# Mean of ReLU over rows: 127 rows a partition in place of 128, the first 128 rows one to a partition

## Chip, cores, metric

One core of one Trainium2 chip. The metric is the device time of one execution in microseconds; the profile's span is some 1.8 us shorter, as it goes from the first to the last instruction. Every run here is of a fast state, with a granted clock of 1.000.

Some words. DVE is VectorE, ACT is ScalarE, POOL is GpSimd. A partition is one of the 128 rows of on-chip memory; the pitch is the distance in HBM between the starts of two neighbouring partitions. A load runs on 16 DMA engines; it has landed when the last of the 16 is done, and its spread is the time from the first of the 16 landings to the last. The last whole row is the last row that is loaded in one piece; one more follows in column pieces. A fetch is a packet of the page's queue of kind "instruction".

## The reference

```python
batch, seq, dim = 32, 512, 1024
x = np.random.randn(batch, seq, dim).astype(np.float32)

def reference(x):
    relu_x = np.maximum(x, 0)
    return np.mean(relu_x, axis=-1).astype(np.float32)
```

So 16,384 rows of 4 KB are read, 64 MB, and one number a row is written.

## The kernel before

Partition p holds the rows 128p to 128p + 127. Seven full tiles of 16 rows a partition (8 MB) are loaded into three buffers. The last 16 rows come in pieces that get smaller, so that little is left to compute after the last landing. ACT takes the even rows and DVE the odd ones, each with an instruction that sums the row as it clips it; POOL scales the sums.

```python
def act_row(nc, src, acc):
    nc.scalar.activation(out=src, in_=src, func=ACT.Relu, accum_out=acc)

def dve_row(nc, src, acc, init=None):
    nc.vector.tensor_scalar(out=src, in0=src, scalar1=0.0, scalar2=init,
                            op0=ALU.max, op1=ALU.add, accum_out=acc)
# ... (the first load is moved ahead of the entry barrier)
    J = R // P                                             # 128
    xr = xf.rearrange("(p j) d -> p j d", p=P, j=J)        # pitch 512 KB
    outr = out.flatten().rearrange("(p j) -> p j", p=P, j=J)
    NB = 16
    full = J // NB - 1                                     # 7
    row_pieces = [8, 4, 2, 1]
    col_pieces = [512, 256, 256]
# ...
    for t in range(full):
        j0 = t * NB
        xt = in_pool.tile([P, NB, D], F32, name="xt")      # bufs=3
        nc.sync.dma_start(out=xt, in_=xr[:, j0:j0 + NB, :])
        rows(xt, 0, NB, j0)
# ... (loads of the last tile: row pieces, then column pieces of the last row)
    for n in row_pieces[:-1]:
        rows(xt, lo, n, j0)
        lo += n
    finish(j0, j0 + lo)
    act_row(nc, prev[:, :512], part[:, 0:1])               # last whole row: two halves
    dve_row(nc, prev[:, 512:], part[:, 1:2])
# ... (POOL adds and scales; the last row by columns, with partial sums chained on DVE)
    nc.sync.dma_start(out=outr, in_=res)
```

Of the kernel before, what the change touches and what calls it, by code (L numbers as in the profile page):

```python
# [1 line left out]

# [4 lines left out]

F32 = mybir.dt.float32
ALU = mybir.AluOpType
ACT = mybir.ActivationFunctionType  # L10
# [9 lines that stand above are left out]
    nc.vector.tensor_scalar(  # L20
        out=src, in0=src, scalar1=0.0, scalar2=init,
        op0=ALU.max, op1=ALU.add, accum_out=acc,
    )


def issue_ahead_of_entry_barrier(nc):


    entry, body = nc.cur_f.blocks[0].instructions, None
    for block in nc.cur_f.blocks[1:]:  # L30
        for k, ins in enumerate(block.instructions):
            if ins.opcode == "DMACopy":
                body, load = block.instructions, k
                break
        if body is not None:
            break
    first = body[load]
    assert first.engine == mybir.EngineType.SP and not first.sync_info.on_wait
    assert all(i.opcode == "DMACopy" or i.engine != first.engine for i in body[:load])
    del body[load]  # L40
    at = next(k for k, i in enumerate(entry) if i.engine == first.engine and i.opcode == "Drain")
    entry.insert(at, first)


@with_exitstack
def kernel(
    ctx: ExitStack,
    tc: tile.TileContext,
    x: bass.AP,
    out: bass.AP,  # L50
):
    nc = tc.nc
    P = nc.NUM_PARTITIONS
    xf = x.flatten_outer_dims()
    R, D = xf.shape
    assert R % P == 0
    J = R // P
    inv = 1.0 / D
    xr = xf.rearrange("(p j) d -> p j d", p=P, j=J)
    outr = out.flatten().rearrange("(p j) -> p j", p=P, j=J)  # L60
    xlast = xr[:, J - 1, :]

    NB = 16
    full = J // NB - 1

    row_pieces = [8, 4, 2, 1]
    assert sum(row_pieces) == NB - 1
    col_pieces = [512, 256, 256]
    assert sum(col_pieces) == D

    pools = ctx.enter_context(ExitStack())
    in_pool = pools.enter_context(tc.tile_pool(name="in", bufs=3))
    res_pool = pools.enter_context(tc.tile_pool(name="res", bufs=1))
    sums = res_pool.tile([P, J], F32)
    res = res_pool.tile([P, J], F32)
    part = res_pool.tile([P, 10], F32)

    def rows(xt, lo, n, j0):

        for k in range(lo, lo + n):  # L80
            j = j0 + k
            (dve_row if j % 2 else act_row)(nc, xt[:, k, :], sums[:, j:j + 1])

    def finish(lo, hi):
        nc.gpsimd.tensor_scalar(  # L85
            out=res[:, lo:hi], in0=sums[:, lo:hi], scalar1=inv, scalar2=0.0, op0=ALU.mult, op1=ALU.add,
        )

    for t in range(full):
        j0 = t * NB  # L90
        xt = in_pool.tile([P, NB, D], F32, name="xt")
        nc.sync.dma_start(out=xt, in_=xr[:, j0:j0 + NB, :])  # L92
        rows(xt, 0, NB, j0)

    j0 = full * NB
    xt = in_pool.tile([P, NB, D], F32, name="xt")
    prev, last = xt[:, NB - 2, :], xt[:, NB - 1, :]
    lo = 0
    for n in row_pieces:
        nc.sync.dma_start(out=xt[:, lo:lo + n, :], in_=xr[:, j0 + lo:j0 + lo + n, :])  # L100
        lo += n
    c = 0
    for w in col_pieces:
        nc.sync.dma_start(out=last[:, c:c + w], in_=xlast[:, c:c + w])
        c += w

    finish(0, j0)
    lo = 0
    for n in row_pieces[:-1]:
        rows(xt, lo, n, j0)  # L110
        lo += n
    finish(j0, j0 + lo)



    act_row(nc, prev[:, :512], part[:, 0:1])
    dve_row(nc, prev[:, 512:], part[:, 1:2])
    nc.gpsimd.tensor_scalar(  # L118
        out=res[:, J - 2:J - 1], in0=part[:, 0:1], scalar1=part[:, 1:2], scalar2=inv, op0=ALU.add, op1=ALU.mult,
    )  # L120
    act_row(nc, last[:, :256], part[:, 2:3])
    dve_row(nc, last[:, 256:512], part[:, 3:4])
    nc.gpsimd.tensor_scalar(  # L123
        out=part[:, 4:5], in0=part[:, 2:3], scalar1=inv, scalar2=0.0, op0=ALU.mult, op1=ALU.add,
    )
    act_row(nc, last[:, 512:640], part[:, 5:6])
    dve_row(nc, last[:, 640:768], part[:, 6:7], init=part[:, 3:4])
    nc.scalar.activation(  # L128
        out=part[:, 7:8], in_=part[:, 5:6], func=ACT.Identity, scale=inv, bias=part[:, 4:5],
    )  # L130
    dve_row(nc, last[:, 768:], part[:, 8:9], init=part[:, 6:7])
    nc.vector.scalar_tensor_tensor(  # L132
        out=res[:, J - 1:J], in0=part[:, 8:9], scalar=inv, in1=part[:, 7:8], op0=ALU.mult, op1=ALU.add,
    )
    nc.sync.dma_start(out=outr, in_=res)

    pools.close()
    tc.close()
    tc.compile()
    issue_ahead_of_entry_barrier(nc)  # L140


# [1 line left out]
_INS = ['x']  # L144
_OUTS = [((32, 512), 'float32')]


# [23 lines left out]
```

## Time and profile before

| | before |
|---|---|
| time, median of 3 | 164.05 us (163.62 to 164.06) |
| DVE, ACT busy | 46%, 43% |
| the 16 DMA engines busy with the loads | 96.6% |
| last landing of x | 158.62 us |
| last instruction of DVE | 159.43 to 159.59 us |
| the store of the result | issued 159.65, landed 161.19 us |

The kernel is one stream of loads with a short end behind it. The lines that carry this stand in the prediction below; what the landings say to a hundredth of a microsecond comes from the semaphore and packet records of the trace, which the views show only through the instructions that wait for them.

### The profile page before, as it was taken

What the parts mean: (1) busy time and instruction counts of PE and PEld (TensorE: products, weight loads), DVE (VectorE), ACT (ScalarE), POOL (GpSimd) and SP (SyncE); (2) the same over time, 40 slices, a digit from 0 to 9 for tenths busy, and PEclk for the clock granted to TensorE, in tenths of its full rate; (3) what the DMA queues carried; (4) which work ended last, traced back from release to release, by engine and by line L of the source; (5) the groups of instructions that cost most, each with busy time, mean ns of one, the idle gap of its engine ahead of it and who ended that gap; (6) DMA issues with size and microseconds to landing.
All of it is one profiled execution on the core that took longest, in us unless ns stands there. A gap on an engine that the chain in (4) does not pass through costs nothing.

```text
span 162.1 us, 358 instructions
## 1 busy us (share of the span) xinstructions
DVE 74.7 (46%) x135; ACT 69.6 (43%) x134; POOL 1.2 (1%) x8
## 2 busy tenths in 40 slices
DVE  0000049700795009930199102990049800698993
ACT  3000049500793009910199002980049600696882
POOL 0000000000000000000000000000000000000001
DMA  8996996997997998998998999899898897998980
GB/s 275 501 485 291 518 501 291 501 501 323 469 518 340 437 518 356 420 518 356 420 520 374 404 501 404 388 501 404 388 518 388 388 518 332 437 445 384 420 311 17
DMA packets 2162, 67.19 MB, mean 415 GB/s; under 512 B 240, under 2 KB 624, under 8 KB 880
## 3 DMA queue, kind: packets, MB, share of 16 engines
q1 hardware_dynamic: 2160, 67.18, 96.6%
q14 instruction: 2, 0.02, 0.0%
HBM read 67.11 MB, written 0.07 MB: 414 GB/s over the span
## 4 chain that ended last, share of the span: by engine, by line
DMA 84%; DVE 13%; SPq 1%; issue 0%; DVEq 0%
DMA xt<-in_x_dram 84%; DVE xt L20 13%; SPq L100 1%; DVE res L132 0%; DVEq L20 0%; DVEq L132 0%; SPq L92 0%
## 5 line engine op out<-in xcount | busy, mean ns | idle before, releaser
L20 DVE TENSOR_SCALAR_CACHE_REDUCE xt<-xt 128x1024 f32<-128x1024 f32 (+1 forms) x65 | 73.7, 1195 | 84.7 <-DMA xt<-in_x_dram 84.3
L15 ACT ACTIVATE xt<-xt 128x1024 f32<-128x1024 f32 (+1 forms) x66 | 67.0, 1015 | 88.7 <-DMA xt<-in_x_dram 88.6
L15 ACT ACTIVATION_READ_ACCUMULATOR xt<-xt 128x1 f32 x66 | 12.3, 186 | 0.0
L20 DVE DVE_READ_ACCUMULATOR xt<-xt 128x1 f32 x65 | 5.4, 83 | 0.0
L85 POOL TENSOR_SCALAR res<-sums 128x112 f32<-128x112 f32 (+1 forms) x2 | 0.5, 252 | 156.7 <-DVE xt L20 156.7
L15 ACT ACT_TABLE_LOAD x1 | 1.3, 1283 | 0.8 <-PEq L155 0.8
L20 DVE TENSOR_SCALAR_CACHE_REDUCE xt<-xt,part 128x128 f32<-128x128 f32 (+1 forms) x2 | 0.8, 412 | 0.1
L128 ACT ACTIVATE part<-part 128x1 f32<-128x1 f32 x1 | 0.3, 294 | 0.1
L118 POOL TENSOR_SCALAR res<-part 128x1 f32<-128x1 f32 x1 | 0.3, 264 | 0.5 <-ACT xt L15 0.5
L132 DVE SCALAR_TENSOR_TENSOR res<-part 128x1 f32<-128x1 f32 x1 | 0.2, 159 | 0.1
L123 POOL TENSOR_SCALAR part<-part 128x1 f32<-128x1 f32 x1 | 0.2, 191 | 0.1
L20 DVE DVE_READ_ACCUMULATOR xt<-xt,part 128x1 f32 x2 | 0.2, 83 | 0.0
L155 POOL MEMSET const-bfloat16-1.0<- 128x1 bf16 x1 | 0.1, 101 | 0.0
L155 POOL MEMSET const-uint8-127<- 128x1 uint8 x1 | 0.1, 101 | 0.0
L155 POOL MEMSET const-float32-0.0<- 128x1 f32 x1 | 0.1, 98 | 0.2 <-issue 0.2
L155 POOL MEMSET const-float32-1.0<- 128x1 f32 x1 | 0.1, 98 | 0.0
## 6 DMA issues: line engine op xcount, KB each, us to landing
xt<-in_x_dram SPq DMA_DIRECT2D x1, 4096.0 KB, 39.0
xt<-in_x_dram SPq DMA_DIRECT2D x1, 2048.0 KB, 43.5
xt<-in_x_dram SPq DMA_DIRECT2D x1, 1024.0 KB, 45.5
xt<-in_x_dram SPq DMA_DIRECT2D x1, 512.0 KB, 46.4
xt<-in_x_dram SPq DMA_DIRECT2D x1, 256.0 KB, 46.5
xt<-in_x_dram SPq DMA_DIRECT2D x2, 128.0 KB, 42.7
xt<-in_x_dram SPq DMA_DIRECT2D x7, 49.1
out_dram<-res SPq DMA_DIRECT2D x1, 64.0 KB, 1.5
```

The costliest lines, as they stand in the source:

```text
L15: nc.scalar.activation(out=src, in_=src, func=ACT.Relu, accum_out=acc)
L20: nc.vector.tensor_scalar(out=src, in0=src, scalar1=0.0, scalar2=init, op0=ALU.max, op1=ALU.add, accum_out=acc,)
L85: nc.gpsimd.tensor_scalar(out=res[:, lo:hi], in0=sums[:, lo:hi], scalar1=inv, scalar2=0.0, op0=ALU.mult, op1=ALU.add,)
L100: nc.sync.dma_start(out=xt[:, lo:lo + n, :], in_=xr[:, j0 + lo:j0 + lo + n, :])
L118: nc.gpsimd.tensor_scalar(out=res[:, J - 2:J - 1], in0=part[:, 0:1], scalar1=part[:, 1:2], scalar2=inv, op0=ALU.add, op1=ALU.mult,)
L123: nc.gpsimd.tensor_scalar(out=part[:, 4:5], in0=part[:, 2:3], scalar1=inv, scalar2=0.0, op0=ALU.mult, op1=ALU.add,)
L128: nc.scalar.activation(out=part[:, 7:8], in_=part[:, 5:6], func=ACT.Identity, scale=inv, bias=part[:, 4:5],)
L132: nc.vector.scalar_tensor_tensor(out=res[:, J - 1:J], in0=part[:, 8:9], scalar=inv, in1=part[:, 7:8], op0=ALU.mult, op1=ALU.add,)
L155: nc = _bacc.Bacc("TRN2", target_bir_lowering=False, num_devices=1)
```

## The change

The 128 rows at the front of x are now one to a partition and are loaded behind the first full tile; the others are 127 to a partition. The starts of the partitions in HBM then lie 508 KB apart rather than 512 KB. That this is the intent is my reading. The first rows get their mean on DVE, with a transpose to bring 128 results from 128 partitions into four rows, and a store of their own on ACT's queue. The last tile has 15 rows instead of 16, in pieces of 8, 4, 1, 1 and the last row.

```diff
-    xr = xf.rearrange("(p j) d -> p j d", p=P, j=J)
-    outr = out.flatten().rearrange("(p j) -> p j", p=P, j=J)
+    outf = out.flatten()
+    M = J - 1
+    xr = xf[P:, :].rearrange("(p j) d -> p j d", p=P, j=M)
+    outr = outf[P:].rearrange("(p j) -> p j", p=P, j=M)
+    xfirst = xf[:P, :]
+    outfirst = outf[:P].rearrange("(q i) -> q i", i=32)
...
-    row_pieces = [8, 4, 2, 1]
+    row_pieces = [8, 4, 1, 1]
...
         rows(xt, 0, NB, j0)
+        if t == 0:
+            x0 = res_pool.tile([P, D], F32)
+            mean0 = res_pool.tile([P, 32], F32)
+            turned0 = res_pool.tile([P, 32], F32)
+            nc.sync.dma_start(out=x0, in_=xfirst)
+            nc.vector.memset(mean0, 0.0)
+            dve_row(nc, x0, mean0[:, 0:1])
+            nc.vector.tensor_scalar_mul(out=mean0[:, 0:1], in0=mean0[:, 0:1], scalar1=inv)
+            nc.vector.transpose(turned0, mean0)
+            nc.scalar.dma_start(out=outfirst, in_=turned0[0:P:32, :])
...
-    for n in row_pieces[:-1]:
+    for n in row_pieces[:2]:
         rows(xt, lo, n, j0)
         lo += n
     finish(j0, j0 + lo)
-    act_row(nc, prev[:, :512], part[:, 0:1])
-    dve_row(nc, prev[:, 512:], part[:, 1:2])
+    for k in range(2):
+        act_row(nc, xt[:, lo + k, :512], part[:, 2 * k:2 * k + 1])
+        dve_row(nc, xt[:, lo + k, 512:], part[:, 2 * k + 1:2 * k + 2])
...  (POOL adds the halves of both rows; the rest renumbers columns)
```

More of the change, by code (lines that the diff above doesn't have):

```diff
@@ L58 @@
     inv = 1.0 / D
-    xr = xf.rearrange("(p j) d -> p j d", p=P, j=J)
-    outr = out.flatten().rearrange("(p j) -> p j", p=P, j=J)
-    xlast = xr[:, J - 1, :]
+    outf = out.flatten()
[4 more added lines that the diff above has]
+    outfirst = outf[:P].rearrange("(q i) -> q i", i=32)
+    xlast = xr[:, M - 1, :]
     NB = 16
-    full = J // NB - 1
-    row_pieces = [8, 4, 2, 1]
-    assert sum(row_pieces) == NB - 1
+    full = M // NB
+    row_pieces = [8, 4, 1, 1]
+    assert full * NB + sum(row_pieces) + 1 == M
     col_pieces = [512, 256, 256]
@@ L73 @@
     res_pool = pools.enter_context(tc.tile_pool(name="res", bufs=1))
-    sums = res_pool.tile([P, J], F32)
-    res = res_pool.tile([P, J], F32)
-    part = res_pool.tile([P, 10], F32)
+    sums = res_pool.tile([P, M], F32)
+    res = res_pool.tile([P, M], F32)
+    part = res_pool.tile([P, 12], F32)
     def rows(xt, lo, n, j0):
@@ L93 @@
         rows(xt, 0, NB, j0)
+        if t == 0:
[8 more added lines that the diff above has]
+            nc.scalar.dma_start(out=outfirst, in_=turned0[0:P:32, :])
     j0 = full * NB
     xt = in_pool.tile([P, NB, D], F32, name="xt")
-    prev, last = xt[:, NB - 2, :], xt[:, NB - 1, :]
+    last = xt[:, NB - 2, :]
     lo = 0
@@ L112 @@
     finish(j0, j0 + lo)
-    act_row(nc, prev[:, :512], part[:, 0:1])
-    dve_row(nc, prev[:, 512:], part[:, 1:2])
+    for k in range(2):
+        act_row(nc, xt[:, lo + k, :512], part[:, 2 * k:2 * k + 1])
+        dve_row(nc, xt[:, lo + k, 512:], part[:, 2 * k + 1:2 * k + 2])
+        nc.gpsimd.tensor_scalar(
+            out=res[:, j0 + lo + k:j0 + lo + k + 1], in0=part[:, 2 * k:2 * k + 1],
+            scalar1=part[:, 2 * k + 1:2 * k + 2], scalar2=inv, op0=ALU.add, op1=ALU.mult,
+        )
+    act_row(nc, last[:, :256], part[:, 4:5])
+    dve_row(nc, last[:, 256:512], part[:, 5:6])
     nc.gpsimd.tensor_scalar(
-        out=res[:, J - 2:J - 1], in0=part[:, 0:1], scalar1=part[:, 1:2], scalar2=inv, op0=ALU.add, op1=ALU.mult,
+        out=part[:, 6:7], in0=part[:, 4:5], scalar1=inv, scalar2=0.0, op0=ALU.mult, op1=ALU.add,
     )
-    act_row(nc, last[:, :256], part[:, 2:3])
-    dve_row(nc, last[:, 256:512], part[:, 3:4])
-    nc.gpsimd.tensor_scalar(
-        out=part[:, 4:5], in0=part[:, 2:3], scalar1=inv, scalar2=0.0, op0=ALU.mult, op1=ALU.add,
-    )
-    act_row(nc, last[:, 512:640], part[:, 5:6])
-    dve_row(nc, last[:, 640:768], part[:, 6:7], init=part[:, 3:4])
-    nc.scalar.activation(
-        out=part[:, 7:8], in_=part[:, 5:6], func=ACT.Identity, scale=inv, bias=part[:, 4:5],
-    )
-    dve_row(nc, last[:, 768:], part[:, 8:9], init=part[:, 6:7])
+    act_row(nc, last[:, 512:640], part[:, 7:8])
+    dve_row(nc, last[:, 640:768], part[:, 8:9], init=part[:, 5:6])
+    nc.scalar.activation(
+        out=part[:, 9:10], in_=part[:, 7:8], func=ACT.Identity, scale=inv, bias=part[:, 6:7],
+    )
+    dve_row(nc, last[:, 768:], part[:, 10:11], init=part[:, 8:9])
     nc.vector.scalar_tensor_tensor(
-        out=res[:, J - 1:J], in0=part[:, 8:9], scalar=inv, in1=part[:, 7:8], op0=ALU.mult, op1=ALU.add,
+        out=res[:, M - 1:M], in0=part[:, 10:11], scalar=inv, in1=part[:, 9:10], op0=ALU.mult, op1=ALU.add,
     )
```

## The prediction

> **What bounds the kernel now.** I read the page first, for who is busy. The two compute engines are at 46% and 43%, while the queue that loads x takes 96.6% of the time of the 16 DMA engines. The chain of work that ended last says the same.
>
> ```profile
> DVE 74.7 (46%) x135; ACT 69.6 (43%) x134; POOL 1.2 (1%) x8
> q1 hardware_dynamic: 2160, 67.18, 96.6%
> DMA 84%; DVE 13%; SPq 1%; issue 0%; DVEq 0%
> ```
>
> The 13% of DVE in the chain is not compute that bounds: the chain leads through buffer reuse, from the release of a buffer to the load that goes into it, and such a load lies behind one or two others in the queue anyway. So I looked next at the timeline of DVE, at the first instruction on each tile, which starts when the tile has landed (columns: start, length, instruction, in brackets how long DVE sat idle before it and for what).
>
> ```profile
> 41.68 1.22 DVE L20 TENSOR_SCALAR_CACHE_REDUCE xt<-xt 128x1024 f32<-128x1024 f32 x1 [10.12 <-DMA xt<-in_x_dram]
> 61.03 1.22 DVE L20 TENSOR_SCALAR_CACHE_REDUCE xt<-xt 128x1024 f32<-128x1024 f32 x1 [10.15 <-DMA xt<-in_x_dram]
> ...
> 100.36 1.22 DVE L20 TENSOR_SCALAR_CACHE_REDUCE xt<-xt 128x1024 f32<-128x1024 f32 x1 [10.64 <-DMA xt<-in_x_dram]
> 119.71 1.22 DVE L20 TENSOR_SCALAR_CACHE_REDUCE xt<-xt 128x1024 f32<-128x1024 f32 x1 [10.15 <-DMA xt<-in_x_dram]
> 139.06 1.22 DVE L20 TENSOR_SCALAR_CACHE_REDUCE xt<-xt 128x1024 f32<-128x1024 f32 x1 [10.14 <-DMA xt<-in_x_dram]
> ```
>
> A tile of 8,388,608 bytes lands every 19.35 us, that is 433.5 GB/s, and DVE idles 10 us in each. One stream of loads, never interrupted, sets the time to about 158.6 us (last landing). Last I read the end, where the stream is over, in the same timeline.
>
> ```profile
> 153.56 1.22 DVE L20 TENSOR_SCALAR_CACHE_REDUCE xt<-xt 128x1024 f32<-128x1024 f32 x1
> 154.70 0.08 DVE L20 DVE_READ_ACCUMULATOR xt<-xt 128x1 f32 x1
> 154.70 1.21 DVE L20 TENSOR_SCALAR_CACHE_REDUCE xt<-xt 128x1024 f32<-128x1024 f32 x1
> 155.84 0.08 DVE L20 DVE_READ_ACCUMULATOR xt<-xt 128x1 f32 x1
> 156.05 1.22 DVE L20 TENSOR_SCALAR_CACHE_REDUCE xt<-xt 128x1024 f32<-128x1024 f32 x1
> 157.19 0.08 DVE L20 DVE_READ_ACCUMULATOR xt<-xt 128x1 f32 x1
> 157.34 0.69 DVE L20 TENSOR_SCALAR_CACHE_REDUCE xt<-xt 128x512 f32<-128x512 f32 x1
> ...
> 157.97 0.42 DVE L20 TENSOR_SCALAR_CACHE_REDUCE xt<-xt 128x256 f32<-128x256 f32 x1
> ...
> 158.83 0.48 DVE L20 TENSOR_SCALAR_CACHE_REDUCE xt<-xt,part 128x256 f32<-128x256 f32 x1
> 158.87 0.29 ACT L128 ACTIVATE part<-part 128x1 f32<-128x1 f32 x1
> 159.23 0.08 DVE L20 DVE_READ_ACCUMULATOR xt<-xt,part 128x1 f32 x1
> 159.43 0.16 DVE L132 SCALAR_TENSOR_TENSOR res<-part 128x1 f32<-128x1 f32 x1
> 159.65 0.35 SPq L135 DMA_DIRECT2D out_dram<-res  x1
> ```
>
> From 157.34, where the last whole row (cut in two halves) has landed, DVE works practically without a gap to 159.59; the column pieces (landed at 157.95, 158.31 and 158.62 by the semaphore records of the trace) meet a DVE that is still busy. So the end hangs on the landing of that row plus the DVE work after it. Before it DVE catches up by 0.1 to 0.2 us on each piece. That is all the slack there is.
>
> **What the Trainium skill says.** (1) "DMA: Bandwidth & Descriptors", section "Latency and other measured facts", on the row pitch in HBM: copies of 128 partitions of 16 KiB with a pitch of 512 KiB a partition ran at 207 GB/s per direction, against 214 with a padded pitch. 128 rows of 4 KB are a pitch of 512 KiB, and 127 rows make it 508 KiB: this is, I think, the intent of the change, and it promises 3%. (2) The same page, "Where 436 GB/s comes from", puts the limit of the 16 ports at 435.2 GB/s, 27.2 a port. The trace sides with the second. The packet records have 64 KB packets at a median of 2418 ns and 32 KB ones at 1213.5; 32,768 bytes in the difference of 1204.5 ns are 27.2 GB/s. The engines already move bytes at the limit of their ports, at the pitch of 512 KiB, so no penalty of the pitch is to be seen that could be removed. (3) The same page, "Why a DMA increments its semaphore by 16 and not by 1": the number of engines that a transfer uses is the largest one up to 16 that divides the slowest dimension of both sides, and 127 partitions would use one engine. Here 127 is the count of rows inside a partition and 128 partitions stay outermost, so I expect 16 engines; before has 16 landings for every load. (4) The same page, "Specifications": under 512 B a transfer takes a read and a write. The last store has 128 packets of 512 B before and of 508 B after. Nothing in the trace of before tests it.
>
> **The change part by part.**
>
> The stream. Row count is the same: 112 + 8 + 4 + 2 + 1 + 1 before, 112 + 1 (first rows, behind tile 0) + 8 + 4 + 1 + 1 + 1 after. A piece of two rows becomes two single ones. By the packet records, an engine takes 8 packets of 311 ns and a 9 ns semaphore write for the two-row piece, 2497 ns; and 8 × 161 + 9 = 1297 ns for a one-row piece, twice 2594. The stream becomes 0.10 us longer. The store of the first 128 results is 4 packets of 128 B, nothing beside the rest, and it lies in the middle.
>
> The work on the first rows. One DVE row (1215 + 83 ns from the groups), a scale on 128x1 (about 159 ns, as the small DVE instruction on line 132), a memset and a 32-wide transpose (an estimate of under 350 ns each, the time of the 128x128 form): some 2 us, in the 10 us that DVE idles after tile 0. ACT issues one DMA and waits for the transpose until about 34 us; its next tile lands near 43. The reuse of tile 0's buffer waits for the tile's own rows, and two tiles are queued ahead of it. Cost 0.
>
> The end. Call X the landing of the last single row: 157.31 + 0.10 = 157.41. The single row before it lands at X − 1.30 and the four-row piece at X − 2.59 = 154.82 (before: 153.54, with 2.49 us to the next piece and 1.28 more to the last row). DVE starts on its two rows of the four at 154.85, and at 1.14 us each it is free at 157.13. Before, by then, the two-row piece and the last row had one whole row in front of X. Now the half of the first single row comes first, 0.63 us (157.34 to 157.97 in the timeline), so DVE is at the last whole row at 157.76, not at 157.34: 0.42 later, of which 0.10 is the stream. The rest, 2.25 us of a DVE that is never idle, follows unchanged. ACT is shorter, 1.04 us a row, and ends in front of it; the extra POOL instruction (264 ns) is off the path.
>
> The store. 508 B packets in place of 512: I add 0.1 for it as a guess between nothing and 1 us. Before, its packets took 27 ns each, and 1.5 us passed from issue to landing.
>
> Sum: 0.10 + 0.32 + 0.1 = about 0.5 us on 164.05: 164.5.
>
> **The rivals.** First, the pitch is a cost and its removal a gain of 2 to 3%. For it: the page of the skill, and the effort that the change makes to get an odd pitch. Against it: the packets are at the rate of the port, and their times hardly vary (2415 lowest, 2418 median). The mean of the 64 KB packets is 2435, so all that lies above the floor is 56 packets an engine × 17 ns, 0.9 us, most of which is the first packet of each engine (about 3.1 us rather than 2.4, the latency of a start). It could make at best 163.5. Second, the store in packets under 512 B becomes read-modify-write in series: 8 packets an engine, an HBM round trip each, would add 1 to 2 us: 165.5 to 166.5. For it, the page; against it, nothing that I have. Third, the new pitch itself reads worse (each 64 KB run now starts at a multiple of 4 KB only): 1% slower packets would add 1.5 us; nothing in the trace speaks for it, as short packets from 1 KB up have the same rate per byte. Fourth, chance in the fetch of instructions. Two such packets of 8 KB at 84.3 and 86.7 us lie between the loads on two of the engines; after them the spread of the 16 landings of a tile grows from 0.83 to 1.34 us and the pace has its one step of 19.85 us. This is worth 0.4 to 0.5 us, and with other instructions it can fall on another engine: either way.
>
> **Range and chances.** The deterministic part is +0.4; store and fetch spread it by some half a microsecond to either side, the three runs of before by 0.4. Eight in ten for 163.9 to 165.4. Faster by 2% would be under 160.8, which is less than the bytes at 433.5 GB/s (154.8 us) plus start and end as they are (2.6 and 5.5 us or more): 1%. Slower by 2% is over 167.3 and needs the store or the pitch to go badly wrong: 3%. Within 2%: 96%.
>
> **What would show it.** The stream: tiles in the middle still land 19.3 to 19.4 us apart and 64 KB packets keep about 2418 ns; if they shorten, the pitch was a cost and I am wrong on what matters most. The end: the half-row instructions on 128x512 come twice, DVE has no idle time between the four-row piece and the last instruction, and the second half-row starts some 0.35 us after its row's landing. The store: 1.5 us from issue to landing now, up to 1.7 after; 2.5 or more means the read-modify-write rival. The first rows: DVE and ACT still idle over 7 us before the second tile. A load that used fewer than 16 engines would show as a tile that takes many times longer, and would make everything above wrong.

## The result

| | before | after |
|---|---|---|
| time, median | 164.01 us (163.62 to 164.06, 4 runs) | 163.83 us (163.77 to 163.95, 4 runs) |
| ratio, 95% interval | | 0.9996 (0.9978 to 1.0013) |

A ratio is the mean time of one kernel's fast runs over the mean of the other's fast runs in the same rounds, so it is not quite the ratio of the medians. The time is the same. I had expected 0.5 us more, and 163.83 is just under the low end of my range (163.9); by the ratio, 0.9996 of the 164.05 that the prediction started from is 163.98, just inside it. The sign of a half microsecond is too small a thing for the class of the result, but where did it go?

The page of the changed kernel: the loads still take nearly all of the DMA engines' time, and the second queue, for the small store, is there with its 8 packets.

```profile
DVE 75.6 (47%) x140; ACT 68.9 (43%) x134; POOL 1.4 (1%) x9
q1 hardware_dynamic: 2304, 67.17, 96.8%
q10 hardware_dynamic: 8, 0.00, 0.0%
```

The timeline of DVE, first instruction on each of the first five tiles after the change:

```profile
22.10 1.22 DVE L20 TENSOR_SCALAR_CACHE_REDUCE xt<-xt 128x1024 f32<-128x1024 f32 x1 [21.15 <-DMA xt<-in_x_dram]
42.73 1.22 DVE L20 TENSOR_SCALAR_CACHE_REDUCE xt<-xt 128x1024 f32<-128x1024 f32 x1 [9.84 <-DMA xt<-in_x_dram]
62.07 1.22 DVE L20 TENSOR_SCALAR_CACHE_REDUCE xt<-xt 128x1024 f32<-128x1024 f32 x1 [10.14 <-DMA xt<-in_x_dram]
81.52 1.22 DVE L20 TENSOR_SCALAR_CACHE_REDUCE xt<-xt 128x1024 f32<-128x1024 f32 x1 [10.25 <-DMA xt<-in_x_dram]
101.23 1.22 DVE L20 TENSOR_SCALAR_CACHE_REDUCE xt<-xt 128x1024 f32<-128x1024 f32 x1 [10.50 <-DMA xt<-in_x_dram]
```

and the two of before that the prediction did not show, the first tile and the one ahead of the slow step:

```profile
22.36 1.22 DVE L20 TENSOR_SCALAR_CACHE_REDUCE xt<-xt 128x1024 f32<-128x1024 f32 x1 [22.36 <-DMA xt<-in_x_dram]
...
80.51 1.22 DVE L20 TENSOR_SCALAR_CACHE_REDUCE xt<-xt 128x1024 f32<-128x1024 f32 x1 [10.27 <-DMA xt<-in_x_dram]
```

The pace between tiles is unchanged (19.34 us from 42.73 to 62.07), and the second tile is 1.31 us later relative to the first, for the load of the first rows. But the first tile lands 0.26 us earlier (22.10 against 22.36), and the one slow step, from the fourth to the fifth tile, is 19.71 us in place of 19.85. By the semaphore records the last tile takes 1.21 us less from its four-row piece to the last whole row (2.57 against 3.78), so the extra packets cost 0.10 us; without these the stream is 0.44 us ahead of before at the last whole row. The end itself, in the same timeline:

```profile
154.43 1.22 DVE L20 TENSOR_SCALAR_CACHE_REDUCE xt<-xt 128x1024 f32<-128x1024 f32 x1
...
155.57 1.21 DVE L20 TENSOR_SCALAR_CACHE_REDUCE xt<-xt 128x1024 f32<-128x1024 f32 x1
...
156.71 0.68 DVE L20 TENSOR_SCALAR_CACHE_REDUCE xt<-xt 128x512 f32<-128x512 f32 x1
...
157.32 0.68 DVE L20 TENSOR_SCALAR_CACHE_REDUCE xt<-xt 128x512 f32<-128x512 f32 x1
...
159.37 0.16 DVE L151 SCALAR_TENSOR_TENSOR res<-part 128x1 f32<-128x1 f32 x1
```

There is no idle time of DVE from 154.43 on, as predicted. The last whole row had landed at 156.97 (semaphore record), and DVE comes to it at 157.32, 0.35 us later. Before, it landed at 157.31 and DVE was there at 157.34. So DVE starts it at the same moment in both: the new end costs 0.35 us, and a stream that is earlier by 0.34 pays for it. The question for the chip is whether the earlier stream is a gain of the change or luck of one trace.

### The profile page after: what moved, and what is told of

Its sections match the earlier page's. It is cut to its first block, busy times and chain, and to the rows that moved or that the text cites. A ratio compares the mean times of both kernels' runs of the same rounds, so it can differ in the third digit from the quotient of the medians.

```text
span 162.0 us, 369 instructions
## 1 busy us (share of the span) xinstructions
DVE 75.6 (47%) x140; ACT 68.9 (43%) x134; POOL 1.4 (1%) x9
## 4 chain that ended last, share of the span: by engine, by line
DMA 83%; DVE 14%; issue 1%; SPq 0%; DVEq 0%
DMA xt<-in_x_dram 83%; DVE xt L20 14%; SPq L117 0%; SPq L105 0%; DVE res L151 0%; DVEq L20 0%; SPq L97 0%; DVEq L151 0%
## 5 line engine op out<-in xcount | busy, mean ns | idle before, releaser
L20 DVE TENSOR_SCALAR_CACHE_REDUCE xt<-xt 128x1024 f32<-128x1024 f32 (+2 forms) x65 | 72.9, 1187 | 82.8 <-DMA xt<-in_x_dram 82.7
L15 ACT ACTIVATE xt<-xt 128x1024 f32<-128x1024 f32 (+2 forms) x66 | 66.5, 1009 | 89.1 <-DMA xt<-in_x_dram 89.1
L20 DVE TENSOR_SCALAR_CACHE_REDUCE x<-x 128x1024 f32<-128x1024 f32 x1 | 1.2, 1219 | 0.0
```

## The experiments

The theories: **A**, the start and the fetch of instructions differ by chance from run to run, and the change costs what I predicted; **B**, the pitch of 512 KB does cost time, and leaving it pays for the new end; **C**, what slows the tile near 90 us is a fetch of instructions on the DMA engines, and how much it costs depends on which engine it meets. Twelve runs were made, each on one chip and with rounds of the kernel before. All were timed in 5 rounds, and every one has the profile of one execution. The traced execution is not always a typical one: where it was the slowest of its run, the text says so. Some give a wrong result, as is said of each.

### Both kernels once more

No edit.

> The kernel before, unchanged, once more. In its first trace the 16 loads of the first tile had all landed at 22.34 us and the last whole row at 157.31. Theory A (start and instruction fetch differ by chance from run to run): another trace of it lands the first tile somewhere between 22.0 and 22.4, and the last whole row between 156.8 and 157.4, not at the same place. Theory B (the pitch of 512 KB makes its start slow): the first tile at 22.3 to 22.4 again. The time against itself: 1.000.

Measured: ratio to itself 0.9998 (0.9985 to 1.0010). First tile at 22.14 us, last whole row at 157.56, the slow step 20.14 us long. The traced execution was the slowest of its five (164.12 us, the median 163.79).

> The changed kernel, unchanged, once more. In its first trace the first tile had landed at 22.08 and the last whole row at 156.97, with DVE only at it at 157.32. Theory A: the first tile anywhere between 22.0 and 22.4. Theory B: at 22.05 to 22.1 again. Both: DVE takes the last whole row some 0.35 us after the landing if that is early, and the ratio to the kernel before is 0.998 to 1.002.

Measured: ratio 1.0004 (0.9992 to 1.0017). First tile at 22.16, last whole row at 157.06, DVE at it at 157.38, 0.32 us late; the slow step 19.68 us.

The first tile of before moved by 0.2 us between two traces, and both first tiles lie outside what B expected and inside what A did (though 157.56 for the last whole row is later than A allowed); single traces cannot tell A from B on the start. That the last whole row lands earlier after the change, by 0.34 us in the first pair of traces, came again, with 0.50; part of that is the slow execution of before.

### The new order at the old pitch

One row of the last tile is loaded behind the first tile and the last tile is cut as after the change; the pitch stays at 512 KB and the store at 512 B. The result is correct.

```diff
-    row_pieces = [8, 4, 2, 1]
+    row_pieces = [8, 4, 1, 1]
...
         rows(xt, 0, NB, j0)
+        if t == 0:
+            x0 = res_pool.tile([P, D], F32)
+            nc.sync.dma_start(out=x0, in_=xr[:, full * NB, :])
+            dve_row(nc, x0, sums[:, full * NB:full * NB + 1])
-    j0 = full * NB
+    j0 = full * NB + 1
...  (the end as in the changed kernel)
```

> The order of loads and the end of the changed kernel, at the old pitch of 512 KB (one row of the last tile is loaded behind the first tile). Theory B, the pitch pays for what the new end costs: first tile at 22.3 to 22.4, ratio to the kernel before 1.002 to 1.003 (the 0.42 us of the prediction). Theory A: as the changed kernel, 0.998 to 1.002. Both: DVE is at the last whole row 0.3 to 0.4 us after it has landed.

Measured: ratio 1.0018 (1.0005 to 1.0032), 0.30 us slower. First tile at 22.31. DVE was at the last whole row at 157.69, 0.35 us after its landing at 157.34. This is the cost that the prediction worked out (0.42, inside the interval of 0.08 to 0.52), seen alone:

```profile
157.69 0.68 DVE L20 TENSOR_SCALAR_CACHE_REDUCE xt<-xt 128x512 f32<-128x512 f32 x1
```

### The pitch alone

The kernel before with the starts of the partitions 127 rows apart. It reads some rows twice, so the result is wrong: the last row of a partition is the first of the next, so the two reads lie at the two ends of the stream. Its instructions stand in the same order on DVE and on the load queue, and its packets have the same sizes.

```diff
-    xr = xf.rearrange("(p j) d -> p j d", p=P, j=J)
+    xr = bass.AP(xf.tensor, 0, [[(J - 1) * D, P], [D, J], [1, D]])
```

> The kernel before with one number changed: the partitions' starts in x lie 127 rows apart, not 128 (so it reads some rows twice and the result is wrong on purpose; every instruction, size and wait is that of before). Theory B, the pitch of 512 KB makes the start slow: in three traces at 512 KB the sixteenth engine's first packet began at 2.16, 2.38 and 2.47 us and the first tile had landed at 22.34, 22.14 and 22.31; in three at 508 KB at 1.66, 1.40 and 1.40, and 22.07, 22.16 and 22.16. Then here the sixteenth first packet begins before 1.7, the first tile lands by 22.2, and the whole is 0.1 to 0.4 us faster than before (ratio 0.9975 to 0.999). Theory A, chance: like before, ratio 1.000, the sixteenth first packet anywhere.

Measured: ratio 0.9974 (0.9961 to 0.9986), 0.42 us faster. **This settles B against A**: one number of the change is worth about what the prediction missed. The profile shows only part of the place. The sixteenth first packet began at 1.69 us, as expected, but the first tile had landed at 22.27, no better than before. The slow step is short in the timeline of DVE:

```profile
80.47 1.22 DVE L20 TENSOR_SCALAR_CACHE_REDUCE xt<-xt 128x1024 f32<-128x1024 f32 x1 [10.27 <-DMA xt<-in_x_dram]
100.07 1.22 DVE L20 TENSOR_SCALAR_CACHE_REDUCE xt<-xt 128x1024 f32<-128x1024 f32 x1 [10.39 <-DMA xt<-in_x_dram]
```

The same two in the repeated kernel before, at 512 KB:

```profile
80.45 1.22 DVE L20 TENSOR_SCALAR_CACHE_REDUCE xt<-xt 128x1024 f32<-128x1024 f32 x1 [10.29 <-DMA xt<-in_x_dram]
100.59 1.22 DVE L20 TENSOR_SCALAR_CACHE_REDUCE xt<-xt 128x1024 f32<-128x1024 f32 x1 [10.93 <-DMA xt<-in_x_dram]
```

19.60 us against 20.14 in that slow execution, and against 19.85 in the first trace of before. A packet of 64 KB took 2418 ns in the median in both kernels, and 2437 in the mean against 2435 and 2436 in the two traces of before, so the gain is not in the time of the packets. This part of the prediction holds.

### A contiguous stream

The seven full tiles as contiguous blocks of 8 MB, so a pitch of 64 KB; the order of rows is wrong.

```diff
+    xb = xf.rearrange("(t p j) d -> t p j d", p=P, j=16)
...
-        nc.sync.dma_start(out=xt, in_=xr[:, j0:j0 + NB, :])
+        nc.sync.dma_start(out=xt, in_=xb[t])
```

> The kernel before with the seven full tiles read as contiguous blocks of 8 MB, so a pitch of 64 KB (wrong order of rows, wrong on purpose; the last tile as before). If what 508 KB does is only to leave the pitch of 512 KB, this start is like that of 508 KB: sixteenth first packet before 1.7 us, first tile by 22.2, ratio as in the run with the pitch alone. If 512 KB is no worse than any other, no difference from before: 1.000. The tiles in the middle stay 19.35 us apart under every theory, as the ports set that.

Measured: ratio 0.9984 (0.9970 to 0.9997), 0.26 us faster. It had the earliest first tile of all (21.92), but its slow step was 20.01 us. The expectation that the tiles in the middle stay 19.35 us apart failed: the second to the fourth landed 19.43, 19.51 and 19.59 us after the one before. (The traced execution was the slowest of its five, 164.14 us, the median 163.75.) So 508 KB is not a lucky pitch; 512 KB is a little worse than two others (the last tile here was still read at 512). How much each of them is worth, these intervals do not separate.

### Few instructions, at both pitches

One instruction of 8 rows for each engine and full tile in place of 8, so that the programs are short; the sums are wrong. Once in the kernel before, once in the changed one.

```diff
-        rows(xt, 0, NB, j0)
+        act_row(nc, xt[:, :8, :].rearrange("p k d -> p (k d)"), sums[:, j0:j0 + 1])
+        dve_row(nc, xt[:, 8:, :].rearrange("p k d -> p (k d)"), sums[:, j0 + 1:j0 + 2])
```

> The kernel before with one instruction of 8 rows an engine for each full tile in place of 8 (the sums are wrong on purpose), so that the programs are too short for a fetch of instructions amid the loads. Theory C, the fetch delays the engine it falls on and the last engine sets every landing: the fetch packets near 85 us are gone, no tile takes over 19.4 us, the spread of the 16 landings stays under 0.9 us to the end, and the kernel is 0.5 to 0.8 us faster (ratio 0.995 to 0.997). If the step in the pace near 90 us has another cause, it stays.

Measured: ratio 0.9967 (0.9955 to 0.9980), 0.54 us faster. The page of before has two packets of instructions:

```profile
q14 instruction: 2, 0.02, 0.0%
```

This line is gone from the page here, and the step with it (timeline of DVE):

```profile
80.60 8.69 DVE L20 TENSOR_SCALAR_CACHE_REDUCE xt<-xt 128x8192 f32<-128x8192 f32 x1 [10.78 <-DMA xt<-in_x_dram]
99.94 8.69 DVE L20 TENSOR_SCALAR_CACHE_REDUCE xt<-xt 128x8192 f32<-128x8192 f32 x1 [10.65 <-DMA xt<-in_x_dram]
```

19.34 us, like any other. **C holds.** The packet records of before show how. They do not name the engines, but an engine's next packet is recorded as starting 3 ns before the end of its last, so that the 16 can be told apart. Two packets of 8 KB and 309 ns, at 84.3 and 86.7 us, each fall on one engine, and the load packet behind each is longer too, 2708 and 3046 ns in place of 2418: the two engines lose 0.60 and 0.94 us. A delayed engine costs only what it lacks in lead over the slowest. The second one had a lead of 0.50 us, which leaves 0.44; the tile landed 0.51 us late, and the spread went from 0.83 to 1.34 us. The delay was not made up: at the last whole row the spread was still 1.33.

> The changed kernel with the same few long instructions (wrong sums on purpose). Theory C: no fetch, no slow tile, 0.3 us faster than the changed kernel (its step was 0.33 us in all three traces at 508 KB, against 0.50, 0.79 and 0.51 at 512 KB). Between this and the run before with few instructions the fetch is out, so what is left is the prediction's sum: 0.10 for the stream, 0.35 for the late DVE, about 0.1 for the store, less what the start gains: 0.3 to 0.5 slower than the other if the start is the same, about 0.3 if the pitch gains 0.15 at the start.

Measured: ratio 0.9983 (0.9970 to 0.9996), 0.28 us faster than the kernel before, and 0.2 to 0.3 faster than the changed kernel itself (0.9996 and 1.0004, in other rounds). Against the run above it is 0.26 us slower: with the fetch out of both, the change costs, though less than the 0.5 of my sum. The first tile landed at 22.00 here and at 22.39 there.

### The pitch alone, with few instructions

The wrong kernel before with few instructions, and the starts 127 rows apart.

```diff
-    xr = xf.rearrange("(p j) d -> p j d", p=P, j=J)
+    xr = bass.AP(xf.tensor, 0, [[(J - 1) * D, P], [D, J], [1, D]])
...  (and one instruction of 8 rows, as above)
```

> The kernel before with few long instructions and the starts of the partitions 127 rows apart (sums wrong on purpose), so the pitch alone where no fetch of instructions falls into the loads. The kernel before with few instructions was 0.9967 of before. If the gain of the pitch of 0.42 us is part start (0.18 us by the landings of the first tile, 22.30 in the mean of five traces at 512 KB against 22.12 in seven at 508) and part a smaller loss to the fetch (0.28), only the start is left here: 0.9956, first tile near 22.1, and 0.2 us between the two. If the fetch has no part in it, the whole gain stays: 0.994. If the start has none either: 0.9967.

Measured: ratio 0.9952 (0.9937 to 0.9967), 0.25 us less than the 0.9967 of its twin (other rounds and another chip, so only roughly). Some gain seems to stay where no fetch is, less than the 0.42, but the two intervals overlap: neither is shown. Its trace is an outlier against the theory of the start: the first tile at 22.46 us, the sixteenth first packet at 2.06. The profiled execution was also the slowest of its six (163.53; the others 162.96 to 163.18).

### Pieces of 7, 4, 2 and 1

The changed kernel with a whole row between the four-row piece and the last whole row, as before the change. Correct.

```diff
-    row_pieces = [8, 4, 1, 1]
+    row_pieces = [7, 4, 2, 1]
...
-    for n in row_pieces[:2]:
+    for n in row_pieces[:-1]:
...
-    for k in range(2):
+    for k in range(1):
```

> The changed kernel with the last tile in pieces of 7, 4, 2 and 1 rows and the last row, in place of 8, 4, 1 and 1: DVE should have caught up when the last whole row lands, and start on it within 0.05 us rather than 0.35. If the late DVE is a cost of the change as I read it, this is 0.3 us faster than the changed kernel (ratio between the two 0.998). If the end is set by the stream alone, no difference.

Measured: ratio 0.9987 (0.9974 to 0.9999), against 1.0004 of the changed kernel in the same rounds: 0.17% or 0.28 us, as expected. The last whole row landed at 157.06, and the timeline of DVE has it there at once:

```profile
155.76 1.22 DVE L20 TENSOR_SCALAR_CACHE_REDUCE xt<-xt 128x1024 f32<-128x1024 f32 x1
...
157.08 0.69 DVE L20 TENSOR_SCALAR_CACHE_REDUCE xt<-xt 128x512 f32<-128x512 f32 x1
```

> The run with pieces of 7, 4, 2 and 1 rows once more, on the chip and in the rounds of the other two. It was 0.9987 of before; again 0.998 to 1.000, with DVE at the last whole row within 0.05 us of its landing.

Measured: ratio 0.9976 (0.9963 to 0.9990); landing 156.96, DVE 156.98. The fix of the end is confirmed twice, and this is the best correct kernel here, some 0.3 us ahead of both.

### The odd store alone

The kernel before with the store of the changed one, 128 packets of 508 B to places 508 B apart. Not all of the output is written.

```diff
-    nc.sync.dma_start(out=outr, in_=res)
+    odd = bass.AP(out.tensor, 0, [[J - 1, P], [1, J - 1]])
+    nc.sync.dma_start(out=odd, in_=res[:, 1:])
```

> The kernel before with the changed kernel's last store: 128 packets of 508 B to places 508 B apart, from columns 1 to 127 (the result is wrong on purpose). In three traces with 508 B the store took 1.59, 1.71 and 1.91 us from issue to landing, in three with 512 B 1.54, 1.55 and 1.54. If the short and unaligned packets cost time, 1.6 to 1.9 us here and 0.05 to 0.3 us slower than before (ratio 1.000 to 1.002); if not, 1.55 us and ratio 1.000.

Measured: ratio 1.0013 (1.0000 to 1.0026), 0.21 us slower (its traced execution was the slowest of its six). The last line of the page, issues with the time to landing, of this run:

```profile
out_dram<-res SPq DMA_DIRECT2D x1, 63.5 KB, 1.8
```

and of the kernel before:

```profile
out_dram<-res SPq DMA_DIRECT2D x1, 64.0 KB, 1.5
```

The traces agree: in seven with 508 B the store took 1.59 to 1.91 us from issue to landing, in seven with 512 B 1.54 or 1.55. So the odd store costs about 0.2 us, though the interval of the time reaches down to nothing. It differs in two things, packets under 512 B and places not aligned to 512 B; this run changes both.

### Few instructions, correct

The kernel with 7, 4, 2 and 1, and for the first five tiles ACT clips 8 rows with one instruction and DVE sums them with one.

```diff
-        rows(xt, 0, NB, j0)
+        if t < full - 2:
+            for h in range(0, NB, 8):
+                nc.scalar.activation(out=xt[:, h:h + 8, :], in_=xt[:, h:h + 8, :], func=ACT.Relu)
+                nc.vector.tensor_reduce(out=sums[:, j0 + h:j0 + h + 8], in_=xt[:, h:h + 8, :],
+                                        axis=mybir.AxisListType.X, op=ALU.add)
+        else:
+            rows(xt, 0, NB, j0)
```

> A correct kernel that joins what the runs so far point to: rows 127 apart, the last tile in pieces of 7, 4, 2 and 1 rows, and for the first five tiles few long instructions (ACT takes 8 rows at a time through the ReLU, DVE sums 8 rows at a time; an estimate from the row times of 1.04 and 1.07 us gives 13 to 14 us of ACT and 17 us of DVE a tile, under the 19.35 of the loads). If few instructions remove the fetch, as in the two runs with wrong sums, no fetch packet lies between 10 and 150 us and it is 0.4 to 0.9 us faster than before (ratio 0.9945 to 0.9975), ahead of the run with 7, 4, 2, 1 alone (0.9987). If the fetch only comes later, it falls into the end and it is no faster than that run.

Measured: ratio 0.9986 (0.9974 to 0.9999), no better than the 0.9976 of the kernel without this, in the same rounds. The fetch did not go away. It came at 152.2 and 152.6 us, and the spread of the landings grew from 0.72 to 1.08 us there. The second of the two outcomes in the expectation is what happened: a fetch that comes late still delays the last engine, if the stream is still running.

## Why the prediction was right or wrong

**The bound and the class**: right. The stream of loads sets the time in every trace, and no part of the change is worth more than 0.3% of the time. That the total is only half a microsecond under the forecast is no merit of the sum: a term of that size was missing, and the width of the range took it in.

**The stream, +0.10**: right. The first rows' load moved the second tile by 1.31 us, where 1.30 was worked out, the last tile saved 1.21, and the paces and the 2418 ns are the same. (Two small readings were off, without effect: the 32 KB packets have a median of 1213 ns, not 1213.5, and short packets do not have quite the same rate per byte, as 1 KB took 46 ns and 64 KB 38 a KB.)

**The late DVE, +0.32**: right in mechanism and size. 0.35, 0.32 and 0.35 us in three traces with one-row pieces at the end, 0.02 in the two where a two-row piece stands in front, and 0.28 us of time between the kernels with and without.

**The first rows, 0**: right. DVE idles 9.84 us before the second tile after the change. The transpose took 213 ns, the scale 154 and the memset 85.

**The store, +0.1**: right in sign as far as the run tells, and about half the measured size; 0.21 us, with an interval from 0.00 to 0.43. The rival of a read and a write in series (1 to 2 us) did not come.

**The pitch, 0**: here the prediction failed. Its words were "no penalty of the pitch is to be seen that could be removed", and in the first rival it set against the gain that "the packets are at the rate of the port, and their times hardly vary". The second is true, and stays true at 508 KB, where the packets are no shorter (mean 2437 ns in the run with the pitch alone, 2435 and 2436 before). But the gain is not in the time of the packets, so that time could neither show nor bound it: "It could make at best 163.5" counts what the packets take above their floor, and leaves out when the 16 engines start and how much lead each has when a fetch falls on it. The sign that the prediction set for this error, shorter packets, would have missed it too. The term should have been −0.42 us. The sum with the measured terms is 0.30 (new order and end) + 0.21 (store) − 0.42 (pitch) = +0.09 us, and the changed kernel measured −0.07 and +0.07: within the intervals, which are 0.2 us or more to either side of each figure, the terms add up. With the fetch out of both kernels they do too: 0.30 + 0.21 − 0.25 is 0.26, and 0.26 was measured, with the same reserve.

**Where the pitch acts** is shown in part. The slow step of the fetch takes 0.51, 0.79, 0.51 and 0.55 us beyond 19.35 in four traces at 512 KB and 0.33, 0.33, 0.32, 0.27 and 0.25 in five at 508 KB, with no overlap, and a mean difference of 0.29 us.

The packets, told apart by engine as above, show more. The engine on which the second fetch packet falls loses about the same at both pitches, 0.88 to 0.94 us at 512 KB and 0.85 to 0.98 at 508, the fetch packet itself included. What differs is the lead that it had over the slowest of the undisturbed engines: 0.22 to 0.50 us in the four traces at 512 KB, 0.63 to 0.66 in the five at 508. This fits the starts. The mean of the 16 first packets' starts was 1.36 to 1.68 us in five traces at 512 KB and 1.11 to 1.19 in eight at 508; these packets ended at 4.44 to 4.60 and 4.34 to 4.43, as the earlier ones took longer. The sixteenth began at 2.02 to 2.47 us in the five and at 1.40 to 1.80 in seven of the eight, with 2.06 in the last; yet the first tile, which waits for the slowest, landed at 22.30 and 22.16 in the mean, with ranges that overlap (22.14 to 22.39, 22.00 to 22.46). So at 508 KB most engines are ahead and the slowest one hardly, and a fetch that falls on another costs less.

This is a reading of traces, not tested by a run of its own, and why the engines start later at 512 KB is open. Two of the five traces at 512 KB also lost 0.12 and 0.16 us on the second to fourth tile, where none at 508 took over 19.36 us a tile. At 64 KB the engines began early (1.14 us in the mean), but the tiles ahead of the fetch were slower and the step was 0.66: not every pitch but 512 KB protects. That something stays without the fetch is what the runs with few instructions suggest (0.25 us), no more.

**The fetch as chance**, the fourth rival: the size was right (0.4 to 0.5 us; 0.54 when removed), the character half wrong, since it favoured one pitch in every trace.

## What to carry to other kernels

When a stream runs at the rate of its ports, ask what it loses at its start and at each interruption, because the last of the 16 engines sets every landing and a delay was not made up here (no full tile took less than 19.32 us in any trace); a cost that the packet times do not show is not thereby zero when the other terms are of a few tenths of a microsecond. After cutting the last pieces differently, add up the compute between them: pieces of 8, 4, 1, 1 left DVE a third of a microsecond behind, and 7, 4, 2, 1 did not. If a change has several parts, run each alone, even when the total is flat: here a gain of 0.42 us lay under two costs of about the same sum (0.30 and 0.21).

## What the Trainium skill lacked or had wrong

- "DMA: Bandwidth & Descriptors", section "Latency and other measured facts", row pitch: it has 207 GB/s for copies at 512 KiB against 214 with a padded pitch, 3%, and nothing on a load from HBM to the on-chip memory. This load, in runs of 64 KB, kept a median of 2418 ns a packet at 512 and 508 KB, and the pitch was worth 0.26% of the time (0.9974), none of it in the time of the packets.
- The same page, "Specifications", transfers under 512 B: no cost is stated. 128 packets of 508 B to unaligned places cost 0.21 us more than 128 of 512 B; the packets themselves took 27 ns both ways, and the landings of the 16 engines spread over 0.17 to 0.50 us rather than 0.17 to 0.18.
- The same page, "Queues, rings and completion order", names a queue row for the runtime's own refills, but no page has what they cost the loads they fall among. Two instruction packets of 8 KB amid the loads cost this kernel 0.54 us of 164, and a correct kernel with 227 instructions in place of 365 only moved them to 152 us.
- No page that I read says that the 16 engines keep the lead or lag of their first packet to the end of a stream at full rate. Here the spread of a tile's landings in before was 0.86 us on the first tile and 0.83 on the fourth, changed by the fetch to 1.34, and 1.33 on the last whole row.
